# Fewer passes for broadcasts, values by transfer in an RWKV scan, alternating expert pieces, single register loads

## The chip, the cores and the metric

The kernel runs on one core of one Trainium2 chip. The metric is the device time of one execution in microseconds. TensorE makes the matrix products, VectorE, ScalarE (ACT) and GpSimd (POOL) the elementwise work, and SyncE (SP) issues most transfers. VectorE is DVE in the rows.

## The reference

Two blocks work on 256 tokens of width 1024 in fp32. The first block has two layers. Layer 0 is an attention and mLSTM mixer with an MLP; layer 1 is an RWKV-7 mixer with an MLP. The second block has a mixer of a gated delta rule (GDN, 8 heads of 128) and a state space model (SSD, 16 heads of 64), and 32 experts of which each token takes 4. What the change touches, cut to its core:

```python
kk = split_heads(k * k_k, RW_HEADS, 64)
kk = kk / jnp.maximum(jnp.linalg.norm(kk, axis=-1, keepdims=True), 1e-12)

def step(s, inp):                       # RWKV-7, once forward, once backward
    rt, wt, kt, vt, at, bt = inp
    sa = jnp.einsum('bhij,bhj->bhi', s, at)
    s = s * wt[..., None, :] + sa[..., None] * bt[..., None, :] + vt[..., None] * kt[..., None, :]
    return s, jnp.einsum('bhij,bhj->bhi', s, rt)

decay = jnp.exp(jnp.where(incl, gam[..., :, None] - gam[..., None, :], -jnp.inf))   # GDN, and alike in SSD
```

An expert is a gated MLP: its first product gives gate and up (1024 to 2 x 1024), both are limited to 7, the gate goes through a sigmoid with factor 1.702, and the second product (1024 to 1024) brings the result back, weighted by the router.

## The kernel before

Most products of weights are made in three passes of split operands: `split` writes a rounded high part and the rest as a low part in the one-pass type fp32r (lines 163 and 164), and lines 242 to 244 multiply them. A product of plain fp32 operands takes four passes and leaves two records in the trace; one of fp32r operands takes one pass and leaves one.

A scheduler orders the instructions of each engine; the program's text gives the order only roughly. Pools of named buffers (`bufs`) and eight PSUM banks, named by tag, set how far a step can run ahead.

**RWKV.** `rw_project` makes k, r and the values v; `v_product` writes v in two tiles of 256 tokens (context and sequence). `rw_prep` (line 1261) broadcasts the 16 rows of key norms `rn` over 128 partitions: two fp32 products with columns of the identity as weights, one for each half of the partitions. There are eight groups (two sequences, four quarters of the heads), and each `rw_prep` does this twice. `rw_scan` runs four steps for a group, two directions at once: the forward one takes chunk n, the backward one chunk 3 - n in reversed order. `load_v` (line 1422) brings the 64 rows of v for both into the buffer `UV`, by products with the identity and with a reversing matrix `J` into a PSUM bank of the scan, and two copies on ACT. It is called for the next step right after the first products of a step, 32 times in all.

**GDN and SSD.** In GDN 24 products (line 1906, three for each of eight heads) broadcast one of 16 rows of 256 numbers to 128 partitions, and VectorE multiplies q or k by the result (lines 1908 and 1911). `decays` (line 1760) broadcasts four rows at a time by four products of 128 columns; line 1763 subtracts, ACT takes the exponential (line 1766). It is called eight times in SSD and four in GDN.

**Experts.** After the router the experts stand in order of their load, in 16 pairs (one expert with many rows, one with few): pair 0 has 64 and 64 rows, pairs 1 to 7 have 96 and 32, pairs 8 to 15 have 64 and 32. An expert of 96 rows is worked in two pieces, 64 and 32. For a piece `up` adds the biases (line 2116), multiplies 8 slices of the input by 8 weight tiles of 1 MB (line 2103) and forms the activated rows `moeu`; `turned` transposes them (line 2135) into `moeaT`; `down` multiplies by 4 weight tiles of 1 MB and scales into `moey` (line 2150). `gather` brings the rows of the next pair together by products with a selection (line 2162), `scatter` adds a finished pair to its tokens (line 2096). SP streams the weights into 16 large buffers, 24 MB for a pair, as buffers come free. Which expert is the r-th is known only at run time: SP loads 30 numbers of `orders` into registers at once (line 2234) and uses them as addresses.

## Time and profile before

| | |
|---|---|
| three runs | 3118.16 us median (3115.72 to 3133.1) |
| the profiled execution | 3121.81 us |
| its span | 3120.0 us |
| mean granted TensorE clock | 0.923 |
| TensorE busy | 2810.8 us (90%) |
| VectorE, ACT, GpSimd busy | 1497.6, 884.1, 492.9 us |
| moved by DMA | 650.76 MB |

The program runs through its stages one after the other: the first layer to about 980 us, the RWKV mixer to 1500, its MLP to 1800, the second block's mixer to 2090, the router and the experts to 3100. A share of the whole span therefore says little; a stage is read from a view cut to its own stretch. In a view by stretch, the granted clock is a share of 2.4 GHz, 0.50 being the lower level, and the DMA share is that of the 16 DMA engines' time. In rows of a single instruction, what stands in brackets is the idle time before it and what ended it. A group of TensorE records can overlap in time, so their sum may be more than the time they take.

### The profile page before, as it was taken

How to read it: one execution, taken by the hardware profiler on the slowest of the kernel's cores; microseconds unless marked ns; L12 is line 12 of the kernel's file. 1: busy time of each engine (PE TensorE's matmuls, PEld its weight loads, DVE VectorE, ACT ScalarE, POOL GpSimd, SP SyncE). 2: the span in 40 equal slices, each digit the busy share in tenths (PEclk: the TensorE clock that was granted, in tenths of full speed). 3: DMA queues.
4: the chain of work that ended last, by engine and by line, in shares of the span. 5: the costliest groups of instructions: out<-in, count | busy, mean ns of one | idle time of the engine just before them, and what ended most of it. 6: DMA issues, size and time to landing. Idle time of an engine off the chain costs nothing. (4 is left out here: it accounts for less than half of the span.)

```text
span 3120.0 us, 47715 instructions
## 1 busy us (share of the span) xinstructions
PE 2810.8 (90%) x19190; PEld 1828.1 (59%) x19190; DVE 1497.6 (48%) x3204; ACT 884.1 (28%) x1824; POOL 492.9 (16%) x753
## 2 busy tenths in 40 slices
PE   7998989999989999887999998989999898887875
PEld 4873468888757666554798967763444333433332
DVE  4426465555567657655656957552222222221222
ACT  4223333222234344324444623541000000000001
POOL 0002211011100534533101212201100000000000
PEclk9999999999988788888999978988999999999987
DMA  6326742323311234342455413367999999999997
GB/s 225 98 98 206 274 135 68 95 95 95 102 56 41 75 112 114 86 126 76 145 187 189 136 30 112 120 250 318 371 413 380 376 377 388 416 417 416 416 417 291
DMA packets 254008, 650.76 MB, mean 209 GB/s; under 512 B 68816, under 2 KB 129616, under 8 KB 215376
## 3 DMA queue, kind: packets, MB, share of 16 engines
q1 hardware_dynamic: 239552, 632.96, 54.9%
q10 hardware_dynamic: 12432, 10.45, 1.1%
q0 software_dynamic: 1792, 4.20, 0.5%
q8 instruction: 153, 2.51, 0.3%
q14 instruction: 79, 0.65, 0.1%
HBM read 639.16 MB, written 8.39 MB: 208 GB/s over the span
## 5 line engine op out<-in xcount | busy, mean ns | idle before, releaser
L2103 PE MATMUL mm<-w,xg 128*32 128x256 f32 (+1 forms) x3904 | 444.1, 460 | 41.7 <-DMA w<-in_moe_w_gu_dram 41.7
L164 DVE TENSOR_TENSOR lo<-w,hi 128x512 fp32r<-128x512 f32 (+1 forms) x330 | 297.2, 934 | 105.0 <-ACT hi L163 90.5
L2103 PEld LDWEIGHTS mm<-w,xg 128*32 128x32 f32 (+1 forms) x3904 | 152.9, 120 | 291.7 <-issue 170.2
L163 ACT ACTIVATE hi<-w 128x512 fp32r<-128x512 f32 (+1 forms) x356 | 256.3, 770 | 231.9 <-PE tp L243 101.1
L2103 PE MATMUL mm<-w,moeaT 128*32 128x256 f32 (+1 forms) x1952 | 238.7, 482 | 11.9 <-ACT moeaT L97 4.7
L2150 DVE TENSOR_TENSOR moey<-mm,moegate 32x256 f32<-32x256 f32 (+1 forms) x122 | 60.5, 496 | 254.5 <-PE mm L2103 253.3
L243 PE MATMUL mm<-mlo,hi 128*128 128x512 f32 (+1 forms) x512 | 173.3, 339 | 0.0
L242 PE MATMUL mm<-mhi,hi 128*128 128x512 f32 (+1 forms) x512 | 173.1, 340 | 0.0
L244 PE MATMUL mm<-mhi,lo 128*128 128x512 f32 (+1 forms) x512 | 172.3, 337 | 0.0
L2103 PEld LDWEIGHTS mm<-w,moeaT 128*32 128x32 f32 (+1 forms) x1952 | 83.2, 126 | 131.9 <-issue 89.0
L2125 ACT ACTIVATE moes<-moeg 128x256 f32<-128x256 f32 (+1 forms) x39 | 19.9, 509 | 478.9 <-DVE moeg L2124 478.9
L244 PE MATMUL tp<-hi,aTl 128*128 128x512 f32 x384 | 151.6, 395 | 0.0
L243 PE MATMUL tp<-lo,aTh 128*128 128x512 f32 x384 | 151.4, 394 | 0.0
L242 PE MATMUL tp<-hi,aTh 128*128 128x512 f32 x384 | 151.0, 393 | 0.0
L2124 DVE TENSOR_SCALAR moeg<-mm 128x256 f32<-128x256 f32 (+1 forms) x39 | 21.1, 541 | 243.0 <-PE mm L2103 242.9
L2127 POOL TENSOR_TENSOR moeg<-moeg,moes 128x256 f32<-128x256 f32 (+1 forms) x39 | 37.4, 959 | 616.1 <-ACT moes L2125 616.1
L164 POOL TENSOR_TENSOR lo<-w,hi 128x512 fp32r<-128x512 f32 (+1 forms) x26 | 51.3, 1974 | 369.6 <-ACT hi L163 313.5
L243 PEld LDWEIGHTS mm<-mlo,hi 128*128 128x128 f32 x512 | 96.4, 188 | 12.0 <-issue 0.5
L242 PEld LDWEIGHTS mm<-mhi,hi 128*128 128x128 f32 x512 | 96.0, 188 | 12.3 <-issue 0.5
L244 PEld LDWEIGHTS mm<-mhi,lo 128*128 128x128 f32 x512 | 96.4, 188 | 11.4
L1319 PE MATMUL pb<-ar,bkT 64*128 64x64 f32 (+1 forms) x512 | 91.5, 323 | 3.4 <-ACT bk L97 2.1
L2098 DVE TENSOR_TENSOR Xl<-Xl,tp 128x512 f32<-128x512 f32 x64 | 42.0, 685 | 108.5 <-PE tp L2096 108.5
(849 smaller groups left out, 5957.4 us busy)
## 6 DMA issues: line engine op xcount, KB each, us to landing
w<-in_moe_w_gu_dram SPq DMA_DIRECT2D x256, 1024.0 KB, 18.7
w<-in_moe_w_down_dram SPq DMA_DIRECT2D x128, 1024.0 KB, 19.8
w<-in_mlp_w_dram SPq DMA_DIRECT2D x64, 1024.0 KB, 5.3
w<-in_ada_w_dram SPq DMA_DIRECT2D x48, 1024.0 KB, 5.8
w<-in_w_in_dram SPq DMA_DIRECT2D x26, 1024.0 KB, 5.3
adaw<-in_ada_w_dram SPq DMA_DIRECT2D x48, 512.0 KB, 4.1
w<-in_ab_w_in_dram SPq DMA_DIRECT2D x14, 1024.0 KB, 5.2
w<-in_rw_w_rkv_dram SPq DMA_DIRECT2D x8, 1024.0 KB, 5.5
```

The costliest lines, as they stand in the source:

```text
L163: nc.scalar.activation(h, raw, AF.Copy)
L164: (eng or nc.vector).tensor_sub(l, raw, hi)
L242: nc.tensor.matmul(out, l[0], r[0], start=start, stop=False)
L243: nc.tensor.matmul(out, l[0], r[1], start=False, stop=False)
L244: nc.tensor.matmul(out, l[1], r[0], start=False, stop=stop)
L1319: nc.tensor.matmul(p[:, n * NT:(n + 1) * NT], bkf[pr_, n].rearrange("p q s -> p (q s)"), A[pr_, n, :], start=True, stop=True)
L2098: nc.vector.tensor_add(x, x, p)
L2103: return 8 * n, lambda p, c, l, r, s, st: nc.tensor.matmul(p[c * n:(c + 1) * n, :8 * n], l, r, start=s, stop=st, tile_position=(0, c * n))
L2124: nc.vector.tensor_scalar(g, pg[:, :w], 7.0, None, op0=OP.min)
L2125: nc.scalar.activation(s, g, AF.Sigmoid, scale=1.702)
L2127: nc.gpsimd.tensor_mul(g, g, s)
L2150: nc.vector.tensor_mul(y[:, cs], py[c * n:(c + 1) * n, :w], gate[c * n:(c + 1) * n, cs])
```

## The change

Four things are changed.

1. **Broadcasts in one pass.** A new helper `stack` writes 16 rows as 48: a rounded high part, 16 rows of zeros, and the low part. The weights are `two16`, a 48 x 16 matrix with ones at both places of a row, so that one fp32r product of 48 rows gives what an fp32 product of 16 gave. It is used for `rn` in RWKV (where GpSimd builds a 128-column selector for each product), and for five sets of rows in GDN and SSD.
2. **The scan's values by transfer.** `v_product` makes v reversed over all 256 tokens, by eight fp32 products with a new `J` after each half of the columns, copies them on VectorE and writes them to DRAM (`vr`). `load_v` is two transfers on ACT's queue, one from v within the chip's buffer, one from `vr`. Its products, its PSUM bank and its copies are gone.
3. **Alternating pieces.** `up` and `down` take both pieces of a 96-row expert together and write their products in turns, of two slices each in both. The gather of the next pair is called with the first expert of a pair, and the scatter of the pair before with the second; before it was the other way round.
4. **Single register loads.** Each expert's number is loaded by itself where it is needed (`moe_expert`).

```diff
+    def stack(self, t, rows):
+        nc = self.nc
+        nc.gpsimd.tensor_scalar(t.bitcast(FR), bc(self.ones[:48, 0:1], list(t.shape)), 0.0, None, op0=OP.mult)
+        nc.scalar.activation(t[0:16].bitcast(FR), rows, AF.Copy)
+        nc.vector.tensor_sub(t[32:48].bitcast(FR), rows, t[0:16])
...
+        self.two16 = cp.tile([48, 16], F32, name="two16")
+        nc.vector.tensor_add(self.two16.bitcast(FR), self.ident[:48, 0:16], self.ident[:48, 32:48])
...
@@ rw_consts @@
-        nc.vector.tensor_scalar(J, J, -127.0, None, op0=OP.add)
-        nc.vector.tensor_mul(J, J, J)
-        nc.vector.tensor_scalar(J, J, 4096.0, None, op0=OP.is_equal)
+        nc.vector.tensor_scalar(J, J, 127.0, None, op0=OP.is_equal)
...
@@ v_product, after each half c of the columns @@
+                for t in range(4):
+                    cs = slice(c * 512, (c + 1) * 512)
+                    p = self.ps("pa")
+                    nc.tensor.matmul(p, rc["J"], v[t // 2][:, t % 2, cs], start=True, stop=True)
+                    st = W.tile([128, 512], F32, name="vrev", tag="bkT", bufs=2)
+                    self.evac(st, p, "v")
+                    nc.sync.dma_start(vr[t // 2][(1 - t % 2) * 128:(2 - t % 2) * 128, cs], st)
...
@@ rw_prep @@
-            for q in range(2):
-                nc.tensor.matmul(pr[q * 64:q * 64 + 64, :256], bc(self.ident[:16, 2 * B + q:2 * B + q + 1], [16, 64]),
-                                 rn[:, ts], start=True, stop=True)
+            sel = T("hsel", 128)[:48]
+            nc.gpsimd.tensor_scalar(sel.rearrange("p (q m) -> p q m", q=2).bitcast(FR),
+                                    bc(self.two16[:, 2 * B:2 * B + 2, None], [48, 2, 64]), 1.0, None, op0=OP.mult)
+            nc.tensor.matmul(pr[:, :256], sel.bitcast(FR), rn[:, ts].bitcast(FR), start=True, stop=True)
...
@@ load_v @@
-            pf = self.ps(sx)
-            for z, sel in ((0, self.ident), (1, rc["J"])):
-                c = n if z == 0 else 3 - n
-                r0 = (c % 2) * 64
-                nc.tensor.matmul(pf[zr[1 - z], :256], sel[:, r0:r0 + 64], v[:, c // 2, hc], start=True, stop=True)
-            for z in range(2):
-                self.evac(UV[zr[1 - z], z, :], pf[zr[1 - z], :256], "s")
+            nc.scalar.dma_start(UV[zr[1], 0, :], v[zr[n % 2], n // 2, hc])
+            nc.scalar.dma_start(UV[zr[0], 1, :], vr[n * 64:(n + 1) * 64, hc])
...
@@ decays, and alike the broadcasts of GDN @@
-            nc.tensor.matmul(p[:, h * 128:(h + 1) * 128], bc(self.ident[:16, r0 + h:r0 + h + 1], [16, 128]),
-                             rows[:, c * 128:(c + 1) * 128], start=True, stop=True)
+            nc.tensor.matmul(p[:, h * 128:(h + 1) * 128], bc(self.two16[:, r0 + h:r0 + h + 1], [48, 128]).bitcast(FR),
+                             rows[:, c * 128:(c + 1) * 128].bitcast(FR), start=True, stop=True)
...
@@ experts, down @@
+                aTs, ps = [turned(u) for u in us], [self.ps("mm") for _ in us]
+                step = 2 if len(us) > 1 else 8
+                for f0 in range(0, 8, step):
+                    for aT, py, y in zip(aTs, ps, ys):
...
@@ experts, the loop over pairs @@
-                    if i == 0:
-                        for _ in back:
-                            pass
-                    elif b < 15:
-                        cur = pair(b + 1)
-                        xn_ = next(cur)
+                    if i == 0 and b < 15:
+                        cur = pair(b + 1)
+                        xn_ = next(cur)
+                    else:
+                        for _ in back:
+                            pass
...
-            _, order = nc.values_load_multi_w_load_instructions(orders[0:1, 2:NE], [mybir.EngineType.SP], min_val=0, max_val=NE - 1)
+    def moe_expert(self, orders, r):
+        if r < 2:
+            return r
+        return self.nc.values_load(orders[0:1, r:r + 1], engines=[mybir.EngineType.SP], min_val=0, max_val=31)
```

The order on the engines, at three places (a number after `x` counts repeats).

**ACT, first group of the scan, before.** `UVs` is the buffer `UV` of a scan, `Xss` the solved rows, `bk` and `E` belong to the preparation of a later group.

```order
L97 ACTIVATE UVs_7834<-s_7837 64x256 x2
L97 ACTIVATE bk<-pb 128x512
L1274 ACTIVATE lw<-pa,rw_hw_5952 128x256
L97 ACTIVATE Xss_7866<-s_7842 128x256
L97 ACTIVATE UVs_7851<-s_7854 64x256 x2
L1275 ACTIVATE av<-pa,rw_ha_5954 128x256
L1276 ACTIVATE lw<-lw,rw_c_5962 128x256
L97 ACTIVATE UVs_7834<-s_7868 64x256
L1281 ACTIVATE E_8354<-cum 128x256
L1288 ACTIVATE wc<-cum 128x4
L1280 ACTIVATE E_8353<-E_8353 128x256
```

**ACT, second and third group of the scan, after.**

```order
L97 ACTIVATE Xss_8191<-s_8172 128x256
L1299 ACTIVATE E_8487<-cum 128x256
L1306 ACTIVATE wc<-cum 128x4
L1298 ACTIVATE E_8486<-E_8486 128x256
L97 ACTIVATE bk<-pb 128x512
L97 ACTIVATE UVs_8091<-s_8193 64x256
L1436 DMA UVs_8534<-v_7464 64x256
L1437 DMA UVs_8534<-vr_7466 64x256
L1292 ACTIVATE lw<-pa,rw_hw_5952 128x256
L1293 ACTIVATE av<-pa,rw_ha_5954 128x256
L1294 ACTIVATE lw<-lw,rw_c_5962 128x256
L97 ACTIVATE Xss_8545<-s_8521 128x256
```

The pairs of copies into `UVs` from the scan's bank `s` are gone, and pairs of transfers from `v` and `vr` stand in their place, among the copies and exponentials of the preparation; the single copies of `UVs` (the scan's own result) stay.

**TensorE, second product of a 96-row expert in a steady pair, before.** `moeaT` are the transposed activated rows (64x512 are products of the 64-row piece, 32x256 of the 32-row piece), `moeu` the activated rows, `moeoh` the gather's selection.

```order
L2135 MATMUL tp<-ident,moeu_19935 128x128 x4
L2103 MATMUL mm<-w,moeaT_20046 64x512 x8
L2135 MATMUL tp<-ident,moeu_20019 128x128 x2
L2162 MATMUL tp<-moeoh,xnmh 128x128 x2
L2103 MATMUL mm<-w,moeaT_20046 64x512 x4
L2103 MATMUL mm<-w,moeaT_20070 32x256 x9
L2103 MATMUL mm<-w,moeaT_20046 64x512 x4
L2103 MATMUL mm<-w,moeaT_20070 32x256 x23
L2116 MATMUL mm<-bguh,moesel 128x256
```

**The same place, after.**

```order
L2169 MATMUL tp<-ident,moeu_19811 128x128 x4
L2122 MATMUL mm<-w,moeaT_19876 64x512
L2169 MATMUL tp<-ident,moeu_19819 128x128 x2
L2122 MATMUL mm<-w,moeaT_19876 64x512 x3
L2122 MATMUL mm<-w,moeaT_19881 32x256 x8
L2122 MATMUL mm<-w,moeaT_19876 64x512 x4
L2122 MATMUL mm<-w,moeaT_19881 32x256 x8
L2122 MATMUL mm<-w,moeaT_19876 64x512 x4
L2122 MATMUL mm<-w,moeaT_19881 32x256 x8
L2122 MATMUL mm<-w,moeaT_19876 64x512 x4
L2122 MATMUL mm<-w,moeaT_19881 32x256 x8
L2140 MATMUL mm<-bguh,moesel 128x256
```

The transposes of the 32-row piece come after one product in place of eight, and the two pieces now alternate to the end. The gather's first products have left this place.

**TensorE, the end of a pair: second product of the 32-row expert, the biases and the first products of the next 96-row expert, before.**

```order
L2116 MATMUL mm<-bguh,moesel 128x256
L2116 MATMUL mm<-bgul,moesel 128x256
L2116 MATMUL mm<-bguh,moesel 128x256
L2116 MATMUL mm<-bgul,moesel 128x256
L2103 MATMUL mm<-w,moeaT_19814 32x256 x24
L2116 MATMUL mm<-bguh,moesel 128x256
L2116 MATMUL mm<-bgul,moesel 128x256
L2116 MATMUL mm<-bguh,moesel 128x256
L2116 MATMUL mm<-bgul,moesel 128x256
L2103 MATMUL mm<-w,xg 64x512 x4
L2103 MATMUL mm<-w,xg 32x256 x8
L2096 MATMUL tp<-moeyh,moegt 128x512
```

**The same place, after.**

```order
L2122 MATMUL mm<-w,moeaT_19604 32x256 x8
L2203 MATMUL tp<-moeoh,xnml 128x128
L2203 MATMUL tp<-moeoh,xnmh 128x128 x2
L2203 MATMUL tp<-moeoh,xnml 128x128 x2
L2203 MATMUL tp<-moeoh,xnmh 128x128 x2
L2203 MATMUL tp<-moeoh,xnml 128x128
L2140 MATMUL mm<-bguh,moesel 128x256
L2140 MATMUL mm<-bgul,moesel 128x256
L2140 MATMUL mm<-bguh,moesel 128x256
L2140 MATMUL mm<-bgul,moesel 128x256
L2203 MATMUL tp<-moeoh,xnml 128x128
L2122 MATMUL mm<-w,xg 64x512 x4
```

The gather (`moeoh`) now lies between the products of this expert and around the last four biases, which in the kernel before wait for the pair's last scaled rows `moey`; the scatter (`moeyh`, `moeyl`) no longer follows the first products of the next expert. The first product of a 96-row expert alternates between its pieces in both orders.

On SP the one load of `orders` stood behind the eight first-product tiles of the second expert. Now two single loads stand behind three of these tiles, ahead of the other five, and one more load stands ahead of each later expert.

## Rows read from the trace of the kernel before

**Rows 1.** Busy by stretch, scan: length; PE, PEld, DVE, ACT, POOL; clock; DMA share, GB/s.
```profile
1100.00:1150.00 50.00, 50.00 (x554) 32.86 (x552) 27.46 (x69) 20.44 (x54) 4.29 (x13) 0.84 0.41 121
...
1400.00:1450.00 50.00, 37.31 (x568) 22.18 (x560) 22.97 (x49) 18.38 (x41) 27.38 (x66) 0.84 0.29 81
```

**Rows 2.** Groups by line, 1810 to 1850 us: busy, mean ns, idle before, releaser.
```profile
L1906 PE MATMUL tp<-grn,ident 16*128 16x256 f32 x32 | 15.8, 615 | 0.0
...
L1906 PE MATMUL tp<-grkb,ident 16*128 16x256 f32 x16 | 8.1, 602 | 0.0
...
L1911 DVE TENSOR_TENSOR KQ<-conv,tp 128x256 f32<-128x256 f32 x16 | 6.6, 420 | 12.1 <-PE tp L1906 12.1
...
L1908 DVE TENSOR_TENSOR conv<-conv,tp 128x256 f32<-128x256 f32 x8 | 3.4, 421 | 7.8 <-PE tp L1906 7.8
```

**Rows 3.** VectorE in order of time: start, length, line, operation, idle before.
```profile
1816.20 0.74 DVE L1911 TENSOR_TENSOR KQ<-conv,tp 128x256 f32<-128x256 f32 x2
...
1846.50 0.42 DVE L1908 TENSOR_TENSOR conv<-conv,tp 128x256 f32<-128x256 f32 x1 [0.50 <-PE tp L1906]
```

**Rows 4.** Busy times by stretch, in the gated delta rule.
```profile
1825.00:1850.00 25.00, 25.00 (x63) 15.96 (x62) 8.46 (x19) 0.00 (x0) 0.00 (x0) 0.50 0.00 0
```

**Rows 5.** Busy times by stretch, experts, first half and second half.
```profile
2412.00:2475.00 63.00, 56.26 (x488) 23.42 (x488) 15.86 (x33) 5.21 (x10) 4.72 (x5) 0.95 0.91 366
2624.00:2675.00 51.00, 44.08 (x360) 20.51 (x352) 13.47 (x30) 4.52 (x8) 3.99 (x4) 0.98 1.02 416
```

**Rows 6.** TensorE in order of time, one load of v and the line behind it.
```profile
1126.82 0.43 PE L1422 MATMUL s<-v,ident 128*64 128x256 f32 x1
...
1127.40 0.66 PE L1327 MATMUL pb<-ident,bkT 128*128 128x128 f32 x4
```

**Rows 7.** Groups by line, 1040 to 1500 us.
```profile
L337 PE MATMUL ad<-adaw,s 128*32 128x512 f32 x192 | 65.3, 683 | 11.9 <-DMA adaw<-in_ada_w_dram 11.9
...
L1422 PE MATMUL s<-v,rw_J 128*64 128x256 f32 x64 | 24.9, 478 | 0.0
...
L1261 PE MATMUL pa<-rn,ident 16*64 16x256 f32 x40 | 12.1, 450 | 0.0
```

**Rows 8.** TensorE in order of time, bias products of an expert.
```profile
2474.54 0.28 PE L2116 MATMUL mm<-bguh,moesel 128*128 128x256 f32 x1
2474.66 0.28 PE L2116 MATMUL mm<-bgul,moesel 128*128 128x256 f32 x1
```

**Rows 9.** DMA issues, 1040 to 1500 us: count, KB each, median us to landing.
```profile
adaw<-in_ada_w_dram SPq DMA_DIRECT2D x48, 512.0 KB, 4.1
...
Ld<-sc SPq DMA_DIRECT2D x50, 32.0 KB, 1.8
```

**Rows 10.** Groups by line, 1750 to 2000 us.
```profile
L1760 PE MATMUL mm<-da,ident 16*128 16x128 f32 x64 | 11.6, 328 | 0.0
...
L1763 DVE TENSOR_TENSOR sE<-mm,scols 128x512 f32<-128x512 f32 x8 | 5.5, 690 | 17.7 <-PE mm L1760 17.7
```

**Rows 11.** TensorE's waits, 2180 to 2600 us: for whom, us in total, times, longest.
```profile
PE tp L2135 <- DVE moeu L2128: 18.9, 11, 2.0
PE mm L2116 <- DVE moey L2150: 9.3, 5, 1.9
PE mm L2103 <- DVE moeaT L95: 3.2, 7, 0.8
PE mm L2103 <- ACT moeaT L97: 2.3, 3, 0.8
```

**Rows 12.** TensorE in order of time, the ends of two following pairs.
```profile
2428.89 0.38 PE L2116 MATMUL mm<-bguh,moesel 128*128 128x256 f32 x1 [1.85 <-DVE moey L2150]
...
2497.05 0.39 PE L2116 MATMUL mm<-bguh,moesel 128*128 128x256 f32 x1 [1.85 <-DVE moey L2150]
```

**Rows 13.** One line of SyncE's: duration ns min/median/max, first and last start us.
```profile
L2234 SPq TENSOR_LOAD <-moeord x1: 6304/6304/6304, 2121.2 to 2121.2; - x1
```

**Rows 14.** DMA issues, the page's part 6, whole program.
```profile
w<-in_moe_w_gu_dram SPq DMA_DIRECT2D x256, 1024.0 KB, 18.7
```

More of the change, by code (lines that the diff above doesn't have):

```diff
@@ L1900, in b2_gdn @@
         kn = kT
+        gg2, rn2, rkb2 = (W.tile([48, 256], F32, name=n + "2", bufs=1) for n in ("ggs", "grn", "grkb"))
+        for t, rows in ((rn2, rn), (rkb2, rkb), (gg2, gg)):
+            self.stack(t, rows)
         KQ = [self.big(f"KQ{i}", 8, 256) for i in range(2)]
@@ L1903, in b2_gdn @@
         for h in range(8):
[L1904 removed]
+            for i, (rows, r, src) in ((1, (rkb2, h, kT)), (2, (rn2, 8 + h, qT)), (0, (rn2, h, kT))):
                 p = self.ps("tp")
[L1906 removed]
+                nc.tensor.matmul(p[:, :256], bc(self.two16[:, r:r + 1], [48, 128]).bitcast(FR), rows.bitcast(FR),
+                                 start=True, stop=True)
                 if i == 0:
@@ L2266, in moe @@
                 pass
-            self.moe_beyond(rows, most, orders, expert, gu_of, dn_of, overflow)
+            self.moe_beyond(rows, most, orders, gu_of, dn_of, overflow)
             self.ln_exp()
```

131 lines of the change are left out of this document (74 added, 57 removed).

## The prediction

> **What bounds the kernel now.** I read the page first, then the busy times by stretch, then the groups by line inside each stretch that the change touches, then single rows in order of time, and the waits last. TensorE is busy for nine tenths of the span in the page's first part, but that figure is a mean over stages with different limits, so each is read by itself. In the RWKV scan (1091 to 1485 us) TensorE is full at the start and slack at the end: 50.00 of 50 us from 1100 on, 37.31 of 50 from 1400 on, while ACT is busy for 20.44 and 18.38 [rows 1]. From 1810 to 1850 us, in the gated delta rule, VectorE waits for TensorE's broadcasts, and TensorE runs at the lower of its two clocks, 1.2 GHz: a granted 0.50 over a stretch in which it was busy for all 25 us [rows 2 to 4]. In the first half of the experts TensorE sets the pace, with DMA at 0.91 of its engines' time; in the second half the weight stream does, at 1.02 and 416 GB/s [rows 5]. Time taken from TensorE is therefore worth something in the scan, most of its size in the gated delta rule and the SSD, something in the first half of the experts and nothing in the second.
>
> **The scan.** *Removed:* 32 loads of two products each. One load stands from 1126.82 us to the next line's start at 1127.40, its two directions at the same time in the two column halves [rows 6]: 0.58 us, so 18.6 us in all, somewhat more at the lower clock; I take 19. The recorded time of one direction alone is 24.9 us [rows 7], which is the upper end.
>
> *Removed:* the broadcast of the key norms, 64 records in all, of which 40 lie in the scan's stretch and take 12.1 us [rows 7], 0.30 each; all 64 make 19.4. In their place come 16 one-pass products of 256 columns. The row nearest to those is the bias product of the experts, one pass of 128x256, where the next begins 0.12 us later [rows 8]: 2 us, and 4 at half the clock. Net 16. Their 16 selectors are built on GpSimd, which is busy for 4.29 and 27.38 of 50 us [rows 1]; they hang on no data and can run ahead. Were they in line, at the 0.42 us of a VectorE operation of like size [rows 2], they would give 7 us back.
>
> *Added:* eight full fp32 products that reverse v (128x512). From below: twice the columns of the bias product [rows 8] and four passes, 8 x 0.24 = 1.0 us each by estimate, 7.7 us together. From above: two records of 0.683 each, the adaln product of the same width [rows 7], 10.9 us. I take 9, nearer to the middle. They stand ahead of the scan, together with eight copies on VectorE and eight writes to DRAM.
>
> So TensorE does 19 + 16 - 9 = 26 us less. The scan is a chain of small steps that also crosses VectorE and ACT, and its end has slack on TensorE, so I count half: **-13**. The ends are -26 and, if the loads hold ACT up, a loss that the first rival prices. ACT gives up 64 copies and issues 64 DMAs instead; I cost this at nothing because ACT is busy for under half of the stretch [rows 1] and each load is issued one step ahead of its use. There are 32 loads in 394 us, one every 12 us, and a 32 KB transfer lands in 1.8 us, one of 512 KB in 4.1 [rows 9].
>
> **The gated delta rule.** 24 broadcasts of 16 rows by 256 columns are 48 records of TensorE, 15.8 + 8.1 = 23.9 us, in a stretch from 1816.2 to 1846.9 us, 31 us long [rows 2, 3]. VectorE needs 0.42 us for each of the 24 products and waited 12.1 + 7.8 = 19.9 us for TensorE in between [rows 2]. With one pass at 0.12 us they cost 2.9. TensorE's remaining work in the stretch is then 31 - 24 + 3 = 10 us, and VectorE's 24 x 0.42 = 10, so both allow a stretch of 11 us, 20 shorter. True fp32 takes four passes through the array, the Trainium skill says ("FP8 and Floating Point Precision", TensorE Precision Notes); by that alone the 23.9 us would fall to 6.0 and not to 2.9, and the gain would be 17 to 18 us. The rows give more because these broadcasts ran mostly at the lower clock. If TensorE stays there, a pass takes 0.24 us and the broadcasts 5.8. The split of the rows into a high and a low part adds a copy and a subtraction on 16 rows in line, about 0.4 us each (the size of VectorE's products here), before the first broadcast; other convolution products cover some of it. I take **-15**, between -20 and -8.
>
> **The decays.** In the SSD 64 records take 11.6 us of TensorE, and VectorE waited 17.7 us for them [rows 10]; the gated delta rule has 32 records of the same form, by estimate 5.8. The new 48 products of 128 columns cost half of 0.12 each, 3 us. So TensorE does 14 us less, in chains that end on VectorE and ACT (the exponentials stay). I take **-8**, between -14 and -3.
>
> **The experts.** *The first product was already alternating:* the order of the kernel before interleaves its 64-row and 32-row pieces, so that part does nothing. *The second product changes.* The 32-row transposes now follow the first 64-row product, where eight stood before. Their waits for the activated rows are worth up to 2.0 us, the longest of 11 [rows 11], so 0 to 2.0 us per pair are added; I take 1.3. *The gather of the next pair moves* from the first product of the 32-row expert into its second. There it covers the wait at the end of a pair, 1.85 us before the last four bias products [rows 12], which five of the pairs in the stretch show with 9.3 us [rows 11]. The scatter moves one expert later and then no longer waits. An idle time also costs clock: 0.95 granted over the 63 us of a pair [rows 5] is a tenth of it at half speed, worth 3 us for three idle times, 1 us each. Per pair: +1.3 - 1.85 - 1 = -1.5, for seven pairs **-10**. The upper end is +6; the lower end is set by the stream, below.
>
> *The register loads.* One load of 30 values held SP for 6.30 us [rows 13]. Thirty single ones cost between 0.2 us (a thirtieth) and 6 each on SP. In the second half 8 transfers are in flight and one lands 18.7 us after its issue [rows 14], which covers even the upper price; in the first half the list of TensorE's waits holds VectorE and ACT, and no transfer [rows 11]. I count nothing. Without that cover 30 x 2 us would be exposed.
>
> **Sum:** -13 - 15 - 8 - 10 = -46 us. The profiled execution took 3121.8 us (span 3120.0), 3.7 above the median of the three runs, 3118.2. So 3075.8 stands beside the profile and **3072** beside the median.
>
> **Rivals.** *1. ACT is held up (slower).* Each of the 64 loads waits on ACT for an earlier transfer, for TensorE's last use of the buffer, or for the write of the reversed values, and the exponentials and copies of the scan stand behind it. The Trainium skill ("DMA: Bandwidth & Descriptors", Anatomy of one DMA) says that a DMA's semaphore wait happens on the sequencer that issues it, which speaks against this change; no run here shows it yet. Price: if each load is exposed with the 1.8 to 4.1 us of the two transfers above, 32 loads cost 58 to 131 us, against a gain of 46. It decides from 1.44 us per load (46 / 32). At 2.0 us the time is 3118 - 46 + 64 = 3136. Against it: the loads are issued ahead, and DMA is not full there (0.41 and 0.29 [rows 1]). Chance 0.07.
>
> *2. TensorE gets shorter, the stages do not.* The scan falls back on its chain through VectorE and ACT (0 in place of -13), and the experts' new wait cancels the old (0 in place of -10): 3118 - 23 = 3095, down to 3106 where the broadcasts too give only their lower ends (-11). For it: TensorE's slack late in the scan. Chance 0.17.
>
> *3. The first half of the experts becomes bound by the stream.* A pair is 24 MB (25.2 million bytes), 60.5 us at 416 GB/s, where a pair now takes 2497.05 - 2428.89 = 68.2 [rows 12]. If the idle times and the clock's losses all went, seven pairs would give 7 x 7.7 = 54, less the 10 already counted: 3028. For it: idle times of 6 to 7 us a pair are all that stands between. Against it: the wait for the activated rows, 18.9 of the 34 us [rows 11], is only moved. Half way there is 3050. Chance 0.12.
>
> *4. The change does nothing that shows* (its parts cancel): 3118. Chance 0.07.
>
> **The numbers.** The forecast, 3050 to 3095 around 3072, has 0.57. The measurement can tell 0.5%, 15.6 us, so faster means below 3102.6: the forecast, rival 3 and most of rival 2, 0.82. Within 0.5%: rival 4 and the rest of rival 2, 0.11. Slower: 0.07. The range from 3034 to 3106 leaves out rivals 1 and 4 and the far end of rival 3.
>
> **What would show it.** In the profile after, the stretch of the broadcasts should be 11 to 20 us long instead of 31, with VectorE hardly waiting. The scan should be 8 to 20 us shorter, with no group of ACT waiting for a transfer by more than 10 us in all. The wait of the biases for the previous pair's rows should be gone from the experts, the wait for the activated rows somewhat longer, and the steady pair should take 66 to 67 us. The second half should stay at 1.02 of the DMA time. I am wrong if ACT's DMA waits show in the scan, or if the steady pair is still 68 us or already 61.

## The result, and the profile after

| | before | after |
|---|---|---|
| median of 16 runs each | 3126.56 us (3115.72 to 3134.76) | 3145.54 us (3125.38 to 3156.76) |
| ratio | | 1.0058, 95% interval 1.0040 to 1.0076 |
| the profiled execution, its span | 3121.81, 3120.0 us | 3129.54, 3127.7 us |
| mean granted TensorE clock | 0.923 | 0.914 |

The change makes the kernel slower by 0.6%. The forecast was 3072 us, a gain of 46. The runs of the changed kernel fall into two halves, eight from 3125 to 3140 us and eight from 3151 to 3157; the profiled execution belongs to the lower half, and what sets the upper one apart took runs of its own (below).

The first reading is by stage. Each boundary is the first or last product of a stage on TensorE, read from the trace in order of time. The second row begins with the first product of the preparation (`rw_prep`); from here on it is called the mixer. All in us, one profiled execution each; the last three columns are experiments that come below.

| stage | before | after | selectors on VectorE | RWKV as before | second block alone |
|---|---|---|---|---|---|
| layer 0, RWKV's products of k, r and the gate | 978.6 | 982.6 | 977.4 | 976.3 | 973.5 |
| RWKV preparation, product of v, scan | 506.5 | 533.8 | 518.3 | 510.1 | 508.9 |
| RWKV output, MLP | 225.6 | 224.0 | 223.8 | 223.8 | 223.9 |
| GDN and SSD | 272.2 | 246.9 | 245.8 | 249.5 | 244.6 |
| end of GDN, output products, router | 126.2 | 126.2 | 124.1 | 134.0 | 124.3 |
| experts | 987.3 | 991.0 | 979.2 | 991.3 | 988.1 |

(The last 23 to 24 us, the end of the program, are left out.) RWKV's first product comes at 871.9 to 878.0 us in these five, behind code that differs in constants alone, so a single row of this table can be trusted to some 6 us at best. From there to the mixer it is 104.5 to 105.6 us in the eleven profiles of kernels with one-pass norms and 101.5 to 102.5 in the five with fp32 norms: some 3 us that the first row hides. GDN and SSD gained 25.3 us, where 23 were forecast (15 + 8) (21 in three later profiles of the changed kernel). The RWKV mixer lost 27.3, where a gain of 13 was forecast. The experts did not gain their 10.

**GDN and SSD came out as forecast.** Groups by line, 1820 to 1900 us of the changed kernel, which answer to [rows 2] (busy, mean ns, idle before, releaser):

```profile
L1930 DVE TENSOR_TENSOR KQ<-conv,tp 128x256 f32<-128x256 f32 x16 | 6.6, 420 | 3.4 <-PE tp L1924 2.8
...
L1924 PE MATMUL tp<-grn,two 48*128 48x256 f32 x16 | 5.9, 374 | 0.4 <-DVE conv L1927 0.2 <-DVE KQ L1930 0.2
...
L1927 DVE TENSOR_TENSOR conv<-conv,tp 128x256 f32<-128x256 f32 x8 | 3.4, 421 | 3.4 <-PE tp L1924 3.4
...
L1924 PE MATMUL tp<-grkb,two 48*128 48x256 f32 x8 | 3.0, 380 | 0.1
```

VectorE's wait for the broadcasts fell from 19.9 to 6.8 us, and the broadcasts' records from 23.9 to 8.9. The stretch now lies from 1847.4 to 1864.4 us and is 17.0 long instead of 30.7. Busy times of that stretch (length; PE, PEld, DVE, ACT, POOL; clock; DMA share, GB/s), beside [rows 4]:

```profile
1847.40:1864.40 17.00, 16.41 (x66) 10.28 (x66) 10.19 (x26) 0.00 (x0) 0.00 (x0) 0.99 0.01 1
```

The clock is at the upper level, where it had been 0.50. The SSD's groups from 1750 to 2000 us answer to [rows 10]:

```profile
L1776 DVE TENSOR_TENSOR sE<-mm,scols 128x512 f32<-128x512 f32 x8 | 5.5, 689 | 8.7 <-PE mm L1773 8.7
L1773 PE MATMUL mm<-da,two 48*128 48x128 f32 x32 | 5.5, 286 | 0.0
```

The records fell from 11.6 to 5.5 us, and VectorE's wait from 17.7 to 8.7.

**The experts changed their waits and kept their time.** TensorE's waits from 2180 to 2600 us, beside [rows 11]:

```profile
PE tp L2169 <- DVE moeu L2161: 17.9, 10, 2.2
PE mm L2140 <- DVE moey L2191: 4.8, 5, 1.5
PE mm L2122 <- DVE moeaT L95: 2.8, 5, 0.8
PE mm L2122 <- ACT moeaT L97: 1.5, 2, 0.7
```

The ends of two following pairs on TensorE, beside [rows 12]:

```profile
2438.48 0.39 PE L2140 MATMUL mm<-bguh,moesel 128*128 128x256 f32 x1 [0.81 <-DVE moey L2191]
...
2506.74 0.39 PE L2140 MATMUL mm<-bguh,moesel 128*128 128x256 f32 x1 [0.81 <-DVE moey L2191]
```

The biases wait 0.81 us instead of 1.85, and the four waits sum to 27.0 us instead of 33.7. Still the pair takes 68.26 us, where it took 68.16. Busy times of that pair, of the kernel before and then of the changed one:

```profile
2428.89:2497.05 68.16, 61.38 (x552) 26.85 (x552) 17.24 (x36) 4.82 (x10) 5.80 (x6) 0.95 0.92 370
```

```profile
2438.48:2506.74 68.26, 62.72 (x553) 27.36 (x553) 16.87 (x36) 4.83 (x10) 5.79 (x6) 0.92 0.93 370
```

TensorE was idle for 1.2 us less, but the same products now take 1.3 us more, at a mean clock of 0.92 in place of 0.95. The stream moved 370 GB/s both times. The other profiles have it alike: in the pair at this place TensorE is busy for 61.4 us at 0.95 in all three kernels with the old loops, and for 62.7 to 62.9 us at 0.92 or 0.93 in all thirteen profiles with the new ones.

**The RWKV mixer is where the time went.** Busy times by stretch, beside [rows 1]:

```profile
1100.00:1150.00 50.00, 48.09 (x702) 34.78 (x702) 35.98 (x93) 24.83 (x66) 2.20 (x4) 1.00 0.42 122
1400.00:1450.00 50.00, 41.35 (x552) 25.52 (x550) 18.95 (x47) 8.99 (x23) 25.24 (x70) 0.90 0.50 139
```

In the first stretch this execution runs ahead of the kernel before: the full clock, 702 products instead of 554, VectorE busy for 36 us instead of 27. But GpSimd is busy for 2.20 of 50 us. It solves the triangular systems of a group (64 operations that write `Tr` or `Tm`), and this is its order of time from 1153 to 1217 us (start, length, line, operation, idle before):

```profile
1153.51 0.78 POOL L1278 TENSOR_SCALAR hsel<-two 48x128 fp32r<-48x128 f32 x1 [17.25 <-PE pa L1280]
1154.24 0.87 POOL L1376 COPY Tr<-L 64x512 f32<-64x512 f32 x1
...
1200.53 0.60 POOL L1376 COPY Tr<-L 64x512 f32<-64x512 f32 x1 [13.56 <-DMA Ld<-sc]
1201.19 0.12 POOL L1385 MEMSET Tr<- 64x16 f32 x1
1214.67 0.58 POOL L1278 TENSOR_SCALAR hsel<-two 48x128 fp32r<-48x128 f32 x1 [13.36 <-PE pa L1280]
1215.30 0.78 POOL L1376 COPY Tr<-L 64x512 f32<-64x512 f32 x1
1216.17 0.29 POOL L1382 TENSOR_TENSOR Tm<-Tr,L 128x30 f32<-128x30 f32 x1
```

A solve begins with its copy at 1200.53. Then comes a selector `hsel` for a later group's broadcast. There are two buffers for selectors, and this one may be overwritten only when TensorE has used it (line 1280). GpSimd stands still for 13.4 us, and the solve behind it with it. The list of GpSimd's waits, 1040 to 1520 us, has it as a group (for whom, us in total, times, longest):

```profile
POOL Tr L1376 <- DMA L<-Ld: 90.2, 5, 27.0
POOL hsel L1278 <- PE pa L1280: 52.0, 5, 17.3
...
POOL hsel L1278 <- PE pa L1290: 22.5, 2, 18.9
```

### The profile page after: what moved, and what is told of

The parts are those of the page before. It is cut to its first block, busy times and chain, and to the rows that moved or that the text cites. A ratio compares the mean times of both kernels' runs of the same rounds, so it can differ in the third digit from the quotient of the medians.

```text
span 3127.7 us, 47385 instructions
## 1 busy us (share of the span) xinstructions
PE 2792.8 (89%) x18958; PEld 1823.1 (58%) x18958; DVE 1500.3 (48%) x3216; ACT 862.4 (28%) x1765; POOL 513.7 (16%) x774
## 5 line engine op out<-in xcount | busy, mean ns | idle before, releaser
L2122 PE MATMUL mm<-w,xg 128*32 128x256 f32 (+1 forms) x3904 | 430.8, 454 | 36.2 <-DMA w<-in_moe_w_gu_dram 36.2
L2122 PE MATMUL mm<-w,moeaT 128*32 128x256 f32 (+1 forms) x1952 | 262.8, 504 | 8.6 <-DVE moeaT L95 4.1
L2158 ACT ACTIVATE moes<-moeg 128x256 f32<-128x256 f32 (+1 forms) x39 | 19.9, 509 | 652.1 <-DVE moeg L2157 652.1
L1337 PEld LDWEIGHTS pb<-ar,bkT 64*128 64x128 f32 x512 | 81.2, 233 | 29.4 <-ACT bk L97 8.5
```

What stands on the lines that cost most here:

```text
L1337: nc.tensor.matmul(p[:, n * NT:(n + 1) * NT], bkf[pr_, n].rearrange("p q s -> p (q s)"), A[pr_, n, :], start=True, stop=True)
L2122: return 8 * n, lambda p, c, l, r, s, st: nc.tensor.matmul(p[c * n:(c + 1) * n, :8 * n], l, r, start=s, stop=st, tile_position=(0, c * n))
L2158: nc.scalar.activation(s, g, AF.Sigmoid, scale=1.702)
```

## The experiments

The suspects in the RWKV mixer were the selectors on GpSimd (theory 1), the loads by transfer (theory 2) and the reversal ahead of the scan (theory 3). Each experiment starts from the changed kernel unless it says otherwise; medians are in us, and ratios are to the kernel before on the same chip.

**Selectors on VectorE.** The other engine builds `hsel`, nothing else differs.

```diff
-            nc.gpsimd.tensor_scalar(sel.rearrange("p (q m) -> p q m", q=2).bitcast(FR),
+            nc.vector.tensor_scalar(sel.rearrange("p (q m) -> p q m", q=2).bitcast(FR),
```

> The changed kernel with the 16 selectors of the norm broadcast built on VectorE, not on GpSimd. Theory 1 (the selectors wait on GpSimd for TensorE and hold back the triangular solve that stands behind them on GpSimd): the scan loses the two long gaps of some 12 us each and the RWKV stage ends 20 to 40 us earlier than in the changed kernel; the whole is 5 to 25 us faster than the kernel before. Theory 2 (the loads of v by transfer hold ACT and the scan up): no change beyond 8 us against the changed kernel, so still 10 to 20 us slower than before.

Measured: 3105.63 (3091.99 to 3119.27, 11 runs) against 3125.75, ratio 0.9941 [0.9919, 0.9964]. One word turns a loss of 0.6% into a gain of 0.6%: 20 us, where theory 1 has 5 to 25. The mixer takes 518.3 us, 15.5 less than in the first profile of the changed kernel; the 20 to 40 less that were expected come only against the later profiles of that kernel (below). GpSimd's order of time at the same solve:

```profile
1207.59 0.60 POOL L1376 COPY Tr<-L 64x512 f32<-64x512 f32 x1 [14.71 <-DMA Ld<-sc]
1208.25 0.12 POOL L1385 MEMSET Tr<- 64x16 f32 x1
1208.58 0.85 POOL L1376 COPY Tr<-L 64x512 f32<-64x512 f32 x1 [0.21 <-DMA L<-Ld]
1209.51 0.29 POOL L1382 TENSOR_TENSOR Tm<-Tr,L 128x30 f32<-128x30 f32 x1
```

The solve runs through: 31 us, 1207.6 to 1238.9, where the changed kernel's takes 44, 1200.5 to 1244.6. More buffers for the selectors, left on GpSimd, would test the wait for a buffer by itself; no run does that.

**Values by products.** The loads are undone (products, copies, the old `J`, no reversal); the selectors stay on GpSimd.

```diff
-                    nc.tensor.matmul(p, rc["J"], v[t // 2][:, t % 2, cs], start=True, stop=True)
...
-            nc.scalar.dma_start(UV[zr[1], 0, :], v[zr[n % 2], n // 2, hc])
-            nc.scalar.dma_start(UV[zr[0], 1, :], vr[n * 64:(n + 1) * 64, hc])
+            pf = self.ps(sx)
...
+                nc.tensor.matmul(pf[zr[1 - z], :256], sel[:, r0:r0 + 64], v[:, c // 2, hc], start=True, stop=True)
```

> The changed kernel with the values loaded by products and copies again (old J, no reversed copy in DRAM), the one-pass norm broadcast with selectors on GpSimd kept. Theory 1: GpSimd still waits for TensorE ahead of the solve, the RWKV stage stays 15 to 30 us longer than in the kernel before, the whole within 10 us of the changed kernel. Theory 2: the RWKV stage falls back to or below the 390 us of the kernel before, the whole is 20 to 35 us faster than before.

Measured: 3132.04 (3111.28 to 3137.67, 12 runs), ratio 1.0015 [0.9995, 1.0035]. The mixer takes 530.0 us, 23.5 more than in the kernel before: that is theory 1's stage, though the whole is 13 us faster than the changed kernel by the ratios, where 10 at most were expected.

**Norms in fp32.** The other half is undone: the norms are broadcast by two fp32 products again, without selectors; the transfers stay.

```diff
-            nc.tensor.matmul(pr[:, :256], sel.bitcast(FR), rn[:, ts].bitcast(FR), start=True, stop=True)
+            for q in range(2):
+                nc.tensor.matmul(pr[q * 64:q * 64 + 64, :256], bc(self.ident[:16, 2 * B + q:2 * B + q + 1], [16, 64]),
+                                 rn[:, ts], start=True, stop=True)
```

> The changed kernel with the key norms broadcast by two fp32 products as before (no selectors, no split), the values still by transfer. Theory 1: the gaps are gone although TensorE has some 16 us more work, the whole is 10 to 30 us faster than before. Theory 2: still slower than before by 10 to 25 us.

Measured: 3125.07 (3116.99 to 3142.9, 12 runs), ratio 1.0007 [0.9987, 1.0026]. The mixer still takes 538.4 us, so the selectors are not the only loss in it. Neither theory has this: 10 to 30 us faster or 10 to 25 slower were expected.

**RWKV as before.** Both halves are undone, by the two diffs above together.

> The changed kernel with both parts in RWKV undone: only the broadcasts of the gated delta rule and the SSD, the alternating pieces and the single register loads are left. Both theories: the second block's mixer gains about 27 us (14 and 13 read from the two profiles) and the experts lose 0 to 5, so 20 to 28 us faster than before. If it is not, the loss lies outside the scan.

Measured: 3102.48 (3089.95 to 3109.99, 6 runs), ratio 0.9922 [0.9895, 0.9950]. The mixer takes 510.1 us. All of the loss comes from it.

**The reversal out of the way, and moved alone.** In the changed kernel the reversing products stand in the bank `pa` and the buffers `bkT`, which the next group's preparation wants. Here they use the scan's banks and a large buffer; the first of the two kernels also builds the selectors on VectorE, the second keeps them on GpSimd.

```diff
-                    p = self.ps("pa")
+                    p = self.ps(tags[t])
...
-                    st = W.tile([128, 512], F32, name="vrev", tag="bkT", bufs=2)
+                    st = self.big("vrev", 1, 512)[:, 0]
```

> The kernel of e1 (selectors on VectorE, values by transfer) with the reversing products in the scan's banks and their copies in a large buffer of their own, so that the preparation of the third group has its banks and its buffers bkT back and stands among the products of v again. Theory 3 (what the transfers cost is one late start: the reversal takes the banks and buffers that the third group's preparation used beside the product of v, and the solve of that group begins 17 us later): that solve begins at 1142 to 1150 us and not at 1159, the whole is 10 to 20 us faster than e1, 30 to 40 faster than before. Theory 2 (each load costs the scan a little): the solve begins early but the later ones fall back, the whole within 6 us of e1.

> The changed kernel with only the reversal moved out of the way as in e5; the selectors stay on GpSimd and hold the solve back. If the two causes add up, 10 to 17 us faster than the changed kernel, so 2 to 8 us slower than before. If GpSimd's waits alone set the pace, no change beyond 5 us: 13 to 23 slower than before.

Measured: with VectorE's selectors 3120.12 (3096.84 to 3132.82, 12 runs), ratio 0.9978 [0.9954, 1.0002]; with GpSimd's 3144.74 (3128.51 to 3151.9, 10 runs), ratio 1.0065 [1.0045, 1.0085]. The mixer takes 521.6 and 555.3 us. The first misses what was expected of the move: by the ratios it is some 12 us slower than with the reversal in its old place (0.9941), their intervals overlapping a little. The second comes out as its other case has it, 20 us slower than before and the same as the changed kernel. The products now use the banks of the scan, and in the first kernel the scan's first product with solved rows (`Xss`) starts at 1118 us, where it started at 1101 with the reversal in its old place. The delay seems to have changed places.

**Products and VectorE's selectors, and the experts as before.** The first takes the values by products and the selectors on VectorE, so that of the RWKV changes only the one-pass norms are left. The second also puts back the experts' loops and the one load of registers.

> Values by products and copies as before, the one-pass norm broadcast with its selectors on VectorE: the transfers undone, GpSimd free. Theory 1 with 3: the third solve begins at 1142 as in e4, none of the solves is longer than 32 us, and the whole is 24 to 35 us faster than before: 0 to 10 us better than e4, 5 to 15 better than e1. Theory 2 makes the same of this kernel; if it is no better than e1, the transfers cost nothing at all.

> The kernel of e6 with the experts of the kernel before (no alternating pieces, registers loaded at once). If the change in the experts does nothing, as a steady pair of 68.3 us against 68.2 says, the whole is within 6 us of e6. If the alternation costs (the low clock lasts longer, 0.92 to 0.94 against 0.94 to 0.95), 5 to 10 us faster than e6. If it gains, 5 to 10 slower.

Measured: 3111.49 (3093.14 to 3119.48, 12 runs) and 3109.99 (3098.6 to 3116.0, 12 runs), ratios 0.9946 [0.9924, 0.9968] and 0.9955 [0.9937, 0.9973] to 3124.73. Two things follow. The experts' change is worth nothing: 1.5 us between the medians, the intervals on top of each other. And the one-pass norms gain nothing: the first kernel was expected to be 24 to 35 us faster than before and is 13, and its mixer takes 514.0 us (513.6 in the second), where the fp32 norms take 510.1. The ratios even make it a loss of some 7 us against RWKV as before (0.9946 and 0.9922, their intervals overlapping), and of 13 us with the old experts (0.9955, against the 0.9912 of the second block alone, below, their intervals just apart).

**No reversal.** The eight products and copies are left out, and v is written to DRAM as it stands, so that the backward direction gets its rows in the wrong order within a chunk. The first kernel has one-pass norms with VectorE's selectors, the second fp32 norms.

```diff
-                    nc.tensor.matmul(p, rc["J"], v[t // 2][:, t % 2, cs], start=True, stop=True)
...
-                    nc.sync.dma_start(vr[t // 2][(1 - t % 2) * 128:(2 - t % 2) * 128, cs], st)
+                    nc.sync.dma_start(vr[t // 2][(t % 2) * 128:(1 + t % 2) * 128, cs], v[t // 2][:, t % 2, cs])
...
-            nc.scalar.dma_start(UV[zr[0], 1, :], vr[n * 64:(n + 1) * 64, hc])
+            nc.scalar.dma_start(UV[zr[0], 1, :], vr[(3 - n) * 64:(4 - n) * 64, hc])
```

> The kernel of e1 (selectors on VectorE, values by transfer) without the reversal: the eight products with J and the eight copies are left out, v goes to DRAM as it is, so the backward scan gets its rows in the wrong order; all transfers stay. Theory 3, as mended after e5 (the reversal is work in series with the start of the scan, wherever it is put; the loads themselves cost nothing): the first Ld of the third group is issued at 1097 to 1102 us and not at 1115, its solve begins by 1147, and the RWKV stage (first product with thw to the first output product) is 506 to 512 us long against 518 in e1 and 514 in e6; the whole 20 to 30 us faster than before. Theory 2 (every load costs): the stage stays at 516 to 520, the whole within 5 us of e1.

> The kernel of e3 (fp32 norms, values by transfer) without the reversal, as in e9 (eight products and copies left out, wrong order of the backward values). Against e4 it differs only in the loads: transfers in place of products and copies. Theory 3: the RWKV stage falls from 538 to 505 to 513 us (510 in e4), the whole is 18 to 28 us faster than before. Theory 2: 525 or more.

Measured: 3111.18 (3106.48 to 3117.55, 6 runs) and 3110.10 (3097.03 to 3128.97, 10 runs), ratios 0.9945 [0.9928, 0.9961] and 0.9951 [0.9926, 0.9976] to 3127.18. The mixer takes 511.7 and 521.3 us, that is 6.6 and 17.1 less than with the reversal. The first is within theory 3's 506 to 512; the second lies between the two theories. The whole kernels are 16 and 17 us faster than before, where 18 to 30 were expected, and against the kernels with the reversal the first gains nothing (0.9945 and 0.9941) and the second 17 us (0.9951 and 1.0007). How the reversal delays the scan can be read from SyncE's order of time: `Ld` belongs to the first solve that GpSimd does in the scan. The changed kernel (with VectorE's selectors this `Ld` comes at 1115.22), then the one without reversal:

```profile
1063.63 6.91 SPq L1247 DMA_DIRECT2D vr<-vrev  x4
1098.32 4.00 SPq L1247 DMA_DIRECT2D vr<-vrev  x4
1115.53 0.81 SPq L1350 DMA_DIRECT2D Ld<-sc  x2
```

```profile
1097.65 0.81 SPq L1346 DMA_DIRECT2D Ld<-sc  x2
```

The last write of reversed rows leaves SyncE at 1102.3 us. From there SyncE waits for VectorE's work on the preparation (13.5 us, put down to `bkT` in its list of waits) before `Ld`, so it is the preparation that comes late, and not the place in SyncE's queue.

**The second block alone.** The kernel before, with the one-pass broadcasts in GDN and SSD and nothing else of the change.

```diff
-                nc.tensor.matmul(p[:, :256], bc(self.ident[:16, r:r + 1], [16, 128]), rows, start=True, stop=True)
+                nc.tensor.matmul(p[:, :256], bc(self.two16[:, r:r + 1], [48, 128]).bitcast(FR), rows.bitcast(FR),
+                                 start=True, stop=True)
```

> The kernel before with one thing of the change only, the one-pass broadcasts of the gated delta rule and the SSD. Read from the stages so far (246 to 250 us against 272 from the first convolution product to the last SSD product) it should be 22 to 26 us faster than before, and within 5 us of e4, which has the changed experts besides. Were the gain given back behind the stage (the experts wait for transfers that do not start earlier), it would show less than 12 us.

Measured: 3100.07 (3088.75 to 3112.47, 6 runs) against 3127.18, ratio 0.9912 [0.9890, 0.9935]: 27 us faster than the kernel before, and faster than the changed one. It has the lowest ratio of all; RWKV as before, with 0.9922, can't be told from it.

**The changed kernel again, three times.** This was to find what sets its upper half of runs apart.

> The changed kernel once more, for a second profile. Its sixteen runs lie in two groups, eight from 3125 to 3140 us and eight from 3151 to 3157, and the profile at hand is of the first (3129.5). Theory A: the slow group loses its time in the RWKV stage, where GpSimd, TensorE and VectorE wait for one another in turn (stage of 545 us or more against 534). Theory B: it loses it where other kernels show two lengths of the same code, between the SSD and the experts (134 us against 124 to 126) and in the output products, by TensorE's lower clock; the RWKV stage stays at 532 to 537.

> As e12, a third profile: whichever group it falls in, its RWKV stage is 532 to 537 us by theory B, and by theory A 532 to 537 in the fast group and 545 or more in the slow one.

> As e12, a fourth profile, so that each group is likely seen at least once: the difference of the two groups stands in the RWKV stage by theory A, behind the SSD by theory B.

Measured: 3159.89, 3148.95 and 3157.22 us, one execution each, all three in or near the upper half, with mixers of 551.3, 552.6 and 552.5 us instead of 533.8. Busy times by stretch, of the first profile of the changed kernel:

```profile
1070.00:1100.00 30.00, 24.67 (x85) 17.04 (x83) 17.60 (x55) 5.56 (x7) 6.22 (x10) 0.89 0.26 79
1100.00:1130.00 30.00, 28.41 (x506) 21.89 (x506) 21.69 (x56) 17.81 (x47) 1.67 (x3) 1.00 0.36 111
```

The same of the first of the three:

```profile
1070.00:1100.00 30.00, 24.79 (x149) 17.08 (x147) 18.50 (x56) 5.66 (x8) 6.24 (x10) 0.94 0.28 88
1100.00:1130.00 30.00, 29.44 (x335) 23.46 (x335) 13.85 (x35) 13.39 (x35) 1.57 (x3) 0.55 0.20 61
```

The program is the same, and in the stretch ahead TensorE is busy for as long. Then, at the scan's start, it is granted 1.00 in the one and 0.55 in the other (0.54 and 0.50 in the other two), and gets through 335 products instead of 506. Of the 30 us between these two profiles, 17.5 lie in the mixer, as theory A has it, and 11.5 behind it, where theory B looked: GDN and SSD take 250.9 us, the row up to the experts 133.7.

**One table for all.** The scan goes from solve to solve, so its time splits in two: from the mixer's first product to the first solve that GpSimd does in the scan, and from there to the start of its last one. From there to the mixer's end it is 82 to 85 us in every kernel. The clock is that from 1100 to 1130 us.

| kernel | reversal | selectors | clock | to first solve | first to last | mixer |
|---|---|---|---|---|---|---|
| before | no | none | 0.73 | 165.9 | 257.2 | 506.5 |
| RWKV as before | no | none | 0.82 | 165.9 | 261.3 | 510.1 |
| products, VectorE's selectors | no | VectorE | 0.79 | 161.0 | 269.9 | 514.0 |
| no reversal | no | VectorE | 0.76 | 158.2 | 270.0 | 511.7 |
| no reversal, fp32 norms | no | none | 0.72 | 161.6 | 274.9 | 521.3 |
| values by products | no | GpSimd | 0.72 | 170.8 | 275.4 | 530.0 |
| norms in fp32 | yes | none | 0.50 | 190.1 | 266.1 | 538.4 |
| selectors on VectorE | yes | VectorE | 0.52 | 181.4 | 252.3 | 518.3 |
| changed | yes | GpSimd | 1.00 | 171.7 | 279.1 | 533.8 |
| changed again, the first | yes | GpSimd | 0.55 | 183.9 | 282.0 | 551.3 |
| reversal moved, VectorE's | moved | VectorE | 0.73 | 175.0 | 263.3 | 521.6 |
| reversal moved, GpSimd's | moved | GpSimd | 0.81 | 181.5 | 289.5 | 555.3 |

- *Selectors on GpSimd* cost 16.0 us where the values come by products (530.0 - 514.0), 33.7 with the reversal moved, and 33.0 with it in place, between the two rows at a like clock (0.55 and 0.52). The ratios say the same: 0.7%, 0.9% and 1.2%, or 22, 27 and 37 us.
- *The reversal* puts the first solve off by 23 us with one-pass norms (181.4 - 158.2). The time from first to last then gets 18 us shorter; 6.6 remain, and 17.1 with fp32 norms. Not all of that need be the reversal's, since the kernels without it also have the higher clock here (0.76 and 0.72 against 0.52 and 0.50); the medians have 0 and 17.
- *The loads by transfer*, with the reversal away, change the mixer by -2.3 us (511.7 - 514.0) or +11.2 (521.3 - 510.1). The ratios say 0 (0.9945 and 0.9946) and 9 us (0.9951 and 0.9922, their intervals overlapping).
- *The low clock at the scan's start* goes, in the changed kernel, with 12 us more to the first solve and 17.5 more in all. No run changes the clock alone.

## Why the prediction was wrong

**The scan: both halves of "so I count half: -13" fell.** TensorE did get most of its relief: the 64 records of loads [rows 7] are gone, and the groups by line, 1040 to 1520 us of the changed kernel, show the other two terms: 7.7 us for the reversal, forecast 9, and 5.1 for 12 of the 16 one-pass products, so some 7 for all, where 2 to 4 were given:

```profile
L347 PE MATMUL ad<-adaw,s 128*32 128x512 f32 x192 | 66.3, 720 | 28.0 <-DMA adaw<-in_ada_w_dram 28.0
...
L1244 PE MATMUL pa<-v,rw_J 128*128 128x512 f32 x16 | 7.7, 601 | 2.6 <-DVE Tm L1382 2.6
...
L1280 PE MATMUL pa<-rn,hsel 48*128 48x256 f32 x12 | 5.1, 421 | 0.7 <-POOL Tm L1382 0.7
```

But the relief was worth nothing. With the selectors off GpSimd, one-pass norms leave the mixer 4 us longer than fp32 ones (514.0 and 510.1), and with the loads taken from TensorE too and no reversal it still takes 511.7. I read "TensorE is full" from 1100 us on and took it for the bound. The scan goes from one solve to the next, 257.2 us for five intervals in the kernel before, some 51 each, of which the solve itself is 28 to 32 on GpSimd; in between GpSimd waits mostly for the next group's rows (`L<-Ld`). That this chain sets the pace is read from the waits; what the runs show is that work taken from TensorE bought nothing, and that a hold on GpSimd cost much. TensorE's longer wait for the weights of the next stage in the first row above, 28.0 us instead of 11.9, goes with the selectors too: it is 24 to 28 us in the six profiles with GpSimd's selectors and 6 to 17 in all others. That the scan's end "has slack on TensorE" was seen, and should have counted for all of it; rival 2 had this at 0.17.

**"They hang on no data and can run ahead" is the step that failed worst.** The selectors need no data, but they need a free buffer. With two buffers the third waits for TensorE's product of the first, and on an engine that works in order it takes the solve along, which is the chain. I priced the selectors at 7 us at most, by their own duration; they cost 16 to 34 in the mixer, and 22 to 37 by the ratios, by what stood behind them. GpSimd's light load [rows 1] was no argument: the engine with 4 of 50 us busy was the one that the chain ran over.

**The reversal was costed as 9 us of TensorE's time, and its place was not costed.** In single profiles it cost the mixer 7 to 17 us, with the first solve put off; between the medians it is nothing beside VectorE's selectors and 17 us beside fp32 norms. Moving it elsewhere did not help, so its banks alone don't explain it; whether the products, the copies among VectorE's operations or the write to DRAM hold the preparation the longest stays open. (In its lower estimate "8 x 0.24" is a slip: the 1.0 us is 8 x 0.12.)

**Rival 1 named the right sign and the wrong engine.** I looked for a wait in a queue, in the one that got the transfers. ACT's waits, 1040 to 1520 us of the changed kernel:

```profile
ACT hl L163 <- DMA UVs<-vr: 12.2, 1, 12.2
...
ACT Xss L97 <- DMA UVs<-vr: 6.0, 3, 2.1
...
ACT lw L1292 <- DMA UVs<-vr: 3.1, 1, 3.1
```

These three groups, five waits, sum to 21.3 us, and one of them is over the 10 I had named as the sign. The 12.2 is a single wait before the scan, where the first four loads stand in ACT's queue until the reversed rows are written. The Trainium skill ("DMA: Bandwidth & Descriptors", Anatomy of one DMA) says that a DMA's wait is served by the sequencer that issues it, and the trace agrees with that 12.2 us. But the scan did not begin later for it (first product with solved rows 124.8 us after the mixer's start, 124.1 before), and the loads themselves are quick. The DMA issues of the same stretch (count, KB each, median us to landing):

```profile
UVs<-v ACTq DMA_DIRECT2D x32, 64.0 KB, 2.3
...
UVs<-vr ACTq DMA_DIRECT2D x32, 64.0 KB, 2.4
```

The rival's price of 58 to 131 us did not come: -2 to +11 were measured. Its form was right, a wait that holds the work queued behind it, and the same question asked of GpSimd would have found the cause.

**The gated delta rule: right, -13.8 for -15** (51.5 to 37.7 us from the first broadcast of `grn` to the last product with `KQ`; the stretch ahead, which now splits the rows, got 1.9 us longer, so 12 remain). I took 2.9 us for the broadcasts and said that a factor of four would leave 6.0. The Trainium skill ("FP8 and Floating Point Precision", TensorE Precision Notes) counts four passes for true fp32. Recorded are 8.9 us, more than either. The passes cannot be read from that: a record of 0.37 is longer than the 0.12 between two starts that I counted with, and the clock differs as well (0.50 before, 0.99 now). The stretch of 17.0 us lies within the 11 to 20 given.

**The decays: right in sign, better in size.** The SSD part fell from 115.5 to 102.4 us, -13.1 for -8, at the far end of its range; in the other profiles with the same code the part takes 101.0 to 107.3 us, so -8 to -14.

**The experts: no gain, and two of the three terms were wrong.** The wait for the activated rows did not grow by "1.3" (18.9 to 17.9 us over the stretch), the biases' wait fell by 1.04 of the 1.85, and "3 us for three idle times" of clock was the wrong way round: TensorE was idle for less and its clock was lower, 0.92 instead of 0.95, and the products took 1.3 us more. The pair stayed where it was, at the 68 us that I had named as a sign of being wrong, and the run with the experts as before confirms that the change is worth nothing.

**The register loads: right.** Row of SyncE (duration min/median/max in ns, first and last start), beside [rows 13]:

```profile
L2318 SPq TENSOR_LOAD <-moeord x30: 264/272/479, 2115.5 to 3055.0; - x30
```

Each takes 0.27 us, close to the lower price of 0.2, and TensorE's waits in the first half still hold no load of weights. In the second half the stream stays at 1.01 of the DMA time:

```profile
2624.00:2675.00 51.00, 45.98 (x376) 22.36 (x372) 13.72 (x29) 4.51 (x8) 3.99 (x4) 0.93 1.01 410
```

**The sum.** Against the 46 us of gain forecast stand about 19 of loss. By the run with RWKV as before, the rest of the change gained 23 us (3125.75 - 3102.48), which is the 46 without the scan's 13 and the experts' 10. The RWKV part lost about 43 (1.0058 - 0.9922 of 3126), where 13 of gain were forecast: by the ratios 22 to 37 of it for the selectors, 0 to 17 for the reversal, 7 to 13 for the one-pass norms with VectorE's selectors and 0 to 9 for the loads. These terms depend on each other and on the clock, and do not add up exactly.

## What to carry to other kernels

Before work is put on an idle engine, ask what is queued behind it there and what it waits for: "no data" is not "nothing", since a buffer that rotates is a wait for its last reader. In a chain of small steps, read which operations follow each other from one round to the next, and price only what shortens those; relief for the full engine beside them bought nothing here. And try the parts of a change alone: here one part's gain of 0.9% stood hidden behind another part's loss.

## What the hardware showed that was not expected

The granted clock of a stretch is not a property of the program alone. The changed kernel was granted 1.00 from 1100 to 1130 us in one profile and 0.50 to 0.55 in three others, after 30 us in which it was busy for 24.7 to 26.1; its 16 runs lie in two halves some 20 us apart. The first 15 us behind the SSD show it too, in two kernels whose code is the same up to there. First of the kernel with products and VectorE's selectors, then of the one that has the experts as before besides:

```profile
1968.20:1983.20 15.00, 15.00 (x161) 12.39 (x161) 3.47 (x5) 5.13 (x10) 1.26 (x1) 0.54 0.21 71
```

```profile
1966.70:1981.70 15.00, 14.44 (x225) 12.36 (x225) 7.53 (x17) 9.02 (x16) 1.26 (x1) 1.00 0.22 72
```

The first gets through 161 products, and its row up to the experts takes 133.6 us; the second through 225, with 124.2. What decides between the two levels no run here shows. A difference of 10 to 20 us between two single profiles of these kernels can therefore be the clock alone, and only the medians of several runs bear a verdict of half a per cent.
